# A hybrid decoder trunk in float32: more input projections multiply high and low tokens as one operand, in a new order, and the group norm's steps come later

## The chip, the cores and the metric

One core of a Trainium2 chip runs the whole kernel. The metric is the device time in microseconds (us), the median of the runs shown; lower is better.

## The reference

Two layers of width 1024 work on a sequence of 256 tokens. Each layer normalises the stream, projects it to 12,832 columns, and feeds three branches of 1024 channels: a Mamba-2 scan, a sliding-window attention and a forgetting attention. Each branch is multiplied by the SiLU of a gate of its own and projected back; the three are merged by sigmoid gates, projected once more and added to the stream.

```python
for layer in range(DEPTH):
    h = rms_norm(x, norm_w[layer])
    proj = einsum('bsd,de->bse', h, w_in[layer])
    (a_xbc, a_z, a_dt, b_q, b_k, b_v, b_z, c_q, c_k, c_v, c_f, c_z, gates) = split(proj)
    y_a = mamba2_branch(a_xbc, a_z, a_dt, ...)      # ends in grouped_rms_norm(y * silu(a_z))
    y_b = sliding_window_branch(rope(b_q), rope(b_k), b_v, b_z, ...)
    y_c = forgetting_attention_branch(c_q, c_k, c_v, c_f, c_z, ...)
    g = sigmoid(gates + gate_bias[layer])
    x = x + einsum(sum_i g_i * (y_i @ w_proj[layer, i]), w_out[layer])
return rms_norm(x, final_norm_w)
```

## The kernel before

**Numbers in two parts.** Everything is float32. So that TensorE can take its faster float32 form (fp32r), each number a is written as a high part, a rounded by ScalarE (ACT), and a low part, a - high, by VectorE (DVE); `split` (lines 261 to 268) does both. A product is then high x high + low x high + high x low, with the product of the two low parts left out.

**Weights.** SyncE loads 512 KB of weights at a time (128 partitions x 1024 columns, a "part") into six raw buffers. `feed` (357) splits a part into `hi` and `lo`, up to four parts ahead of TensorE (PE), and `release` (377) lets the next one in. A piece of 256 output columns is two parts: four of the eight 128-row blocks k each (`kper` is 4). It gives two blocks of 128 channels, u or half 0 and 1.

**Two ways to multiply 128 channels with 256 tokens.** The normalised tokens stand in `y.hT`, high and low side by side; `y.hTh` and `y.hTl` are views of its halves.
- `chan` (443) does for each of eight k three matmuls of 256 columns into one half of a PSUM bank: `hi` with the high tokens, `lo` with the high tokens, `hi` with the low tokens (`dense`, 278). That is 24 matmuls. The callers read the result from PSUM.
- `chan_sum` (450) loads `hi(k)` once and streams high and low tokens as one operand of 512 columns, so that the bank holds hi x high in the first half and hi x low in the second; `lo(k)` with the high tokens is added into the first half. That is 16 matmuls. Then ACT copies the second half to SBUF (line 463) and DVE adds the first (464). Its matmuls alternate: high 0, low 0, low 1, high 1, low 2, high 2 and so on.

`chan_sum` serves the queries of the sliding window but for the first group (`u_bq`, 536, through `rotated`, 499), the keys and queries of the forgetting attention (`u_ck`, `u_cq`), all its gates, and the first four gate blocks of branch 1 (`u_z`, 813). `chan` serves the sliding keys (`u_bk`), the first queries (g = 0), gate blocks u = 4 to 7 of branch 1, all eight gate blocks of the scan (branch 0) and the convolution's inputs.

**What is done with them.** `rotated` multiplies each half with the cosine and sine table (513), POOL adds or subtracts. `u_z` makes a SiLU: tanh of half the value on ACT (831, or 821 after `chan_sum`), then DVE's (1 + tanh) x value (834, 838, 823). For the scan, DVE then multiplies it with the scan's output `y.xs` (839), ACT squares it (841), and each second block adds two squares (844) and launches a group norm.

**The group norm** (849) has two steps on PE. The first sums the squares over channels with four small matmuls against `ones` (852); DVE, POOL and DVE again make the reciprocal root (854 to 866); ACT writes it as diagonal matrices (`diagonals`, 872). That writing is hung on the next `finish`, that is behind the next block's ACT instruction. The second step broadcasts the diagonals with two matmuls (882), DVE scales (885), and `split` makes the operand of the branch's projection.

**What sets the order.** PE's order is the order in which the program issues it. A modelled clock adds up matmul columns; multi-step work (`launch`, 103) waits in a list until its due time on that clock, and `pump` (130), called after each block, lets due steps in. The group norm's first step is due `D_GN1` after its gate block, the second `D_GN2` after the first. `drain` forces what is left of a branch's steps. The order on ACT, DVE and POOL is made by a scheduler from dependencies; each engine then runs its queue in that order. PSUM has three banks for these products ("mm") and five for the rest ("mx").

**Order of a layer.** Values, sliding keys, four groups of queries; branch 1's gates, the convolution's inputs and the forgetting attention's values, with attention steps in between; branch 1's merge gates and projection; more keys, queries and gates; then the scan's eight gate blocks u0 to u7, four blocks of merge gates (24 matmuls of 512 columns each), and the scan's projection, which needs the group norms.

Of the kernel before, what the change touches and what calls it, by code (L numbers as in the profile page):

```python
# [16 lines left out]
P = 128  # L17
# [6 lines left out]

D_SOFT, D_SOFT2, D_EVAC, D_SSD, D_SSD2 = 7.0, 3.0, 3.0, 8.0, 3.0
D_K, D_Q, D_QK, D_G0, D_FOX, D_BDMA, D_BIAS, D_BC, D_SSD3 = 6.0, 5.5, 2.0, 8.0, 0.0, 4.0, 2.6, 5.5, 1.0
D_GN1, D_GN2, D_CUM, D_H, D_M = 6.0, 9.0, 12.0, (4.8, 6.4), 5.0
BUDGET = 1.35
T_PP, T_SSD, T_BIAS = 1, 1, 1
N_RAW, N_SPLIT = 6, 6  # L30
# [14 lines left out]
def hybrid_trunk(  # L45
# [45 lines left out]
    def mm(o, a, b, **kw):  # L91
        n = b.free_size()
        if a.dtype == F32R:
            clock["t"] += max(0.094, n / 2350.0)
        else:
            clock["t"] += max(0.2, n / 587.0) * (0.5 if a.free_size() == 64 or a.shape[0] == 32 else 1.0)
        nc.tensor.matmul(o, a, b, **kw)  # L97
# [149 lines left out]
    def tokens_in_turn(a, k):  # L247
        return a[:, :, k, :].rearrange("p a i -> p i a")
# [5 lines left out]
    def halves(ap):  # L254

        return ap.rearrange("p (a i) -> p a i", a=2)
# [193 lines left out]
    def chan_sum(y, w, c, out):  # L450


        p = pmm()
        for k in range(NK):
            if k > 0:
                mm(p[:, 0:S], w.lo(k)[:, c:c + P], tokens_in_turn(y.hTh, k), start=False, stop=False)
            mm(p, w.hi(k)[:, c:c + P], y.hT[:, :, :, k, :].rearrange("p h a i -> p h i a"),
               start=(k == 0), stop=(k == NK - 1))
            if k == 0:
                mm(p[:, 0:S], w.lo(k)[:, c:c + P], tokens_in_turn(y.hTh, k), start=False, stop=False)  # L460
            if w.last and (k + 1) % w.kper == 0:
                release(w, k // w.kper + 1)
        finish(act(halves(out), ordered(p[:, S:2 * S]), AF.Copy))  # L463
        tt(halves(out), ordered(p[:, 0:S]), halves(out), op=ALU.add)  # L464

# [30 lines left out]

    def rotated(y, done, both):

        held = {}

        def u(half):
            def f(w):
                if both:
                    p = T("L1", [P, S])
                    chan_sum(y, w, half * P, p)
                    p = halves(p)
                else:
                    p = chan(y, w, half * P)  # L510
                for i in (half, 1 - half):
                    m = held[half, i] = T("L1", [P, S])
                    tt(halves(m), p, halves(cs[:, i, :]), op=ALU.mult)
                if half == 1:
                    done(held)
                pump()
            return f
        return u(0), u(1)
# [6 lines left out]
    def u_bk(y):  # L525

        def done(held):
            y.kT = T("L8", [P, 4, 2, S])
            add_rotated(y.kT[:, 0, :, :], held)
            for d in range(1, 4):  # L530
                m = 32 * d
                nc.gpsimd.dma_start(y.kT[m:P, d, :, :], y.kT[0:P - m, 0, :, :])
                nc.gpsimd.dma_start(y.kT[0:m, d, :, :], y.kT[P - m:P, 0, :, :])
        return rotated(y, done, False)

    def u_bq(y, g):

        def done(held):
            q = T("qt", [P, 2, S])
            add_rotated(q, held)  # L540
            launch(1, swa_quad(y, g, q), D_Q)
        return rotated(y, done, g > 0)

    def attn_quad(pair, products, biases, nsink, v, vcols, sz, gated, scored=lambda: None):

# [267 lines left out]
    def u_z(y, br, u, c):  # L813
        def f(w):
            if u == 0 and br != 0:
                y.sz[br] = T("L8", [P, NK, S])
            if br == 2 or br == 1 and u < 4:
                o = y.sz[br][:, u, :]
                chan_sum(y, w, c, o)
                th = T("L1", [P, S])  # L820
                act(th, o, AF.Tanh, scale=0.5)
                y.zdone.add((br, u))
                stt(o, th, 1.0, o, op0=ALU.add, op1=ALU.mult)
                pump()
                return
            p = chan(y, w, c)
            if u == 0 and br == 0:
                y.yh[br] = T("L8", [P, 2, NK, P], F32R)
                y.yl[br] = T("L8", [P, 2, NK, P], F32R)
            th = T("L1", [P, S])  # L830
            finish(act(halves(th), p, AF.Tanh, scale=0.5))
            y.zdone.add((br, u))
            if br != 0:
                stt(halves(y.sz[br][:, u, :]), halves(th), 1.0, p, op0=ALU.add, op1=ALU.mult)
            else:
                drain(0)
                sz = T("L1", [P, S])
                stt(halves(sz), halves(th), 1.0, p, op0=ALU.add, op1=ALU.mult)
                tt(y.xs[:, u, :], y.xs[:, u, :], sz, op=ALU.mult)
                sq = T("L1", [P, S])  # L840
                act(sq, y.xs[:, u, :], AF.Square)
                y.sq.append(sq)
                if u % 2 == 1:
                    tt(y.sq[-2], y.sq[-2], y.sq[-1], op=ALU.add)
                    launch(3 if u < 4 else 4, group_norm(y, u // 2, y.sq[-2]), D_GN1)
            pump()
        return f
# [596 lines left out]
```

## Time and profile before

| what | value |
|---|---|
| runs | 832.01, 829.56, 830.33 us; median 830.33 |
| the profiled execution | 830.05 us, of it span 828.2 (first to last instruction) |
| granted TensorE clock | 0.997 |
| ACT busy | 522.7 us (63%) |
| POOL busy | 97.3 us (12%) |
| HBM | 154.63 MB read, 189 GB/s over the span |

A row of groups reads: line of the kernel, engine, operation, written <- read, shapes, count; then busy time, mean ns of one, and the idle time of the engine ahead of it with what ended it. A matmul's duration is its way through the array, so that matmuls overlap; what one costs in a stream is the distance from start to start. A timeline row begins with start and length in us. PEld is the loading of weights, beside the matmuls.

### The profile page before, as it was taken

Reading aid. Unit: us, or ns where it says so; the run is one execution under the profiler, and the core shown is the slowest. Engines: PE = TensorE matmul, PEld = TensorE weight load, DVE = VectorE, ACT = ScalarE, POOL = GpSimd, SP = SyncE. Lnnn points to the kernel's source line nnn. Section 1 sums busy time; section 2 is a strip of 40 time slices with the busy share of each in tenths; the row PEclk is TensorE's granted clock in tenths of the full one; section 3 lists DMA queues with packets and bytes.
Section 4 is the critical chain, followed back from the end, with each engine's and each line's share of the span. In section 5 each row is a group of like instructions: output and inputs, shape, how many; then the busy total and the mean of one; then the engine's idle time right before and its main releaser. Section 6 shows DMA issues by size and latency. Waiting matters only on the chain.

```text
span 828.2 us, 15796 instructions
## 1 busy us (share of the span) xinstructions
PE 818.4 (99%) x5781; PEld 743.7 (90%) x5781; DVE 676.0 (82%) x1486; ACT 522.7 (63%) x1082; POOL 97.3 (12%) x150
## 2 busy tenths in 40 slices
PE   8999999999999999999999999999999999999996
PEld 8989999988888998888999999989888889888896
DVE  6998998797997778665788989988889778795665
ACT  7767777664676767353664687767557667664442
POOL 3340000000111010210004200000002110103000
PEclk9999999999999999999999999999999999999998
DMA  9876555766655555775688455756756555476632
GB/s 312 266 206 187 164 159 152 239 214 197 191 172 172 154 167 177 251 241 184 211 269 257 131 174 176 205 158 204 248 174 196 179 167 156 136 230 228 216 104 74
DMA packets 129558, 159.38 MB, mean 192 GB/s; under 512 B 7970, under 2 KB 98202, under 8 KB 129482
## 3 DMA queue, kind: packets, MB, share of 16 engines
q1 hardware_dynamic: 114960, 140.53, 54.1%
q10 hardware_dynamic: 13690, 16.24, 6.6%
q0 software_dynamic: 832, 1.62, 0.7%
q8 instruction: 45, 0.74, 0.4%
q14 instruction: 31, 0.25, 0.1%
HBM read 154.63 MB, written 2.16 MB: 189 GB/s over the span
## 4 chain that ended last, share of the span: by engine, by line
PE 90%; DVE 4%; issue 2%; DMA 2%; ACT 1%; SPq 0%; POOLq 0%; POOL 0%; DVEq 0%; ACTq 0%
PE mm L97 79%; PE mx L97 8%; PE mx L101 4%; DVE lo L265 1%; DMA L<-cumd 1%; DMA L<-in_x_dram 1%; DVE L L723 0%; ACT hi L264 0%; DVE L L265 0%; ACT L L872 0%; DVE pp L567 0%; DVE L L259 0%; DVE L L774 0%; DVE lo L259 0%; DVE pp L585 0%
## 5 line engine op out<-in xcount | busy, mean ns | idle before, releaser
L97 PE MATMUL mm<-L,hi 128*128 128x256 f32 (+1 forms) x1568 | 362.1, 316 | 0.0
L265 DVE TENSOR_TENSOR lo<-raw,hi 128x1024 fp32r<-128x1024 f32 (+2 forms) x276 | 314.8, 1157 | 51.9 <-ACT hi L264 48.6
L264 ACT ACTIVATE hi<-raw 128x1024 fp32r<-128x1024 f32 (+2 forms) x276 | 265.8, 980 | 96.0 <-PE mm L97 83.5
L97 PE MATMUL mm<-hi,L 128*128 128x512 f32 (+2 forms) x1232 | 323.7, 352 | 0.6 <-DVE qt L464 0.4
L97 PE MATMUL mm<-L,lo 128*128 128x256 f32 x1056 | 278.3, 274 | 0.0
L97 PEld LDWEIGHTS mm<-L,hi 128*128 128x128 f32 x1568 | 258.5, 191 | 18.1 <-issue 5.1
L97 PEld LDWEIGHTS mm<-hi,L 128*128 128x128 f32 x1232 | 216.7, 190 | 24.3 <-issue 0.7
L97 PE MATMUL mm<-lo,L 128*128 128x512 f32 (+2 forms) x616 | 213.7, 349 | 0.0
L97 PEld LDWEIGHTS mm<-L,lo 128*128 128x128 f32 x1056 | 202.5, 192 | 2.8
L97 PEld LDWEIGHTS mm<-lo,L 128*128 128x128 f32 x616 | 116.4, 190 | 11.5
L936 POOL TENSOR_SCALAR_AFFINE_SELECT bias<-bias 128x128 f32<-128x128 f32 x64 | 31.0, 520 | 394.9 <-DMA bias<-cumd 377.3
L573 ACT ACTIVATE pp<-pp,nm 128x128 f32<-128x128 f32 (+1 forms) x128 | 56.5, 443 | 17.2 <-DVE nm L567 17.2
L723 DVE SCALAR_TENSOR_TENSOR L<-L,vec,L 128x255 f32<-128x255 f32 (+2 forms) x96 | 46.2, 481 | 3.8 <-ACT L L720 2.5
L585 DVE TENSOR_SCALAR pp<-pp,rsum 128x128 f32<-128x128 f32 (+1 forms) x128 | 32.2, 315 | 0.5
L463 ACT ACTIVATE L<-mm 128x256 f32<-128x256 f32 x36 | 13.7, 381 | 26.5 <-PE mm L97 26.0
L967 ACT ACTIVATE L<-L 128x512 f32<-128x512 f32 x24 | 15.1, 628 | 20.4 <-DVE L L966 20.4
L604 ACT ACTIVATE L<-mx 128x512 f32<-128x512 f32 x48 | 26.7, 596 | 0.3
L101 PE MATMUL mx<-ident,pp 128*128 128x128 f32 x192 | 26.3, 273 | 0.0
L727 ACT ACTIVATE L<-L 128x256 f32<-128x256 f32 x32 | 13.4, 418 | 18.6 <-DVE L L723 10.6
L966 DVE TENSOR_TENSOR L<-mm,L 128x512 f32<-128x512 f32 x24 | 16.4, 684 | 9.4 <-PE mm L97 8.2
L573 ACT ACTIVATION_READ_ACCUMULATOR pp<-pp,nm 128x1 f32 x128 | 24.0, 187 | 0.0
L567 DVE CUSTOM_DVE_ANT_0 pp<-mx,wmask,nsink 128x128 f32<-128x128 f32 x64 | 23.4, 411 | 0.0
(203 smaller groups left out, 767.4 us busy)
## 6 DMA issues: line engine op xcount, KB each, us to landing
raw<-in_w_in_dram SPq DMA_DIRECT2D x191, 512.0 KB, 4.7
raw<-in_w_proj_dram SPq DMA_DIRECT2D x48, 512.0 KB, 5.1
raw<-in_w_out_dram SPq DMA_DIRECT2D x16, 512.0 KB, 5.0
bias<-cumd ACTq DMA_DIRECT2D x16, 256.0 KB, 3.6
L<-cumd ACTq DMA_DIRECT2D x8, 512.0 KB, 8.0
L<-in_gate_bias_dram ACTq DMA_DIRECT2D x12, 256.0 KB
raw<-in_w_in_dram SPq DMA_DIRECT2D x4, 408.0 KB
raw<-in_w_in_dram SPq DMA_DIRECT2D x4, 384.0 KB
```

Of the source, the lines that this page charges most:

```text
L97: nc.tensor.matmul(o, a, b, **kw)
L101: nc.tensor.transpose(o, a, i)
L264: keep(act)(hi, src, AF.Copy)
L265: keep(tt)(lo, src, hi.bitcast(F32), op=ALU.subtract)
L567: nc.vector.tensor_tensor_reduce(out=pp[:, i, sl], in0=score(p, i, b), in1=biases(p, i, b), scale=-0.125, scalar=1.0e30 if ns is None else ...
L573: act(pp[:, i, sl], pp[:, i, sl], AF.Exp, scale=-1.0, bias=nm[:, e:e + 1], accum_out=sums[:, e:e + 1])
L585: ts(pp[:, i, sl], pp[:, i, sl], rs[:, 2 * i + b:2 * i + b + 1], 0.5, op0=ALU.mult, op1=ALU.mult)
L604: act(pT, pt, AF.Copy)
L723: stt(a[:, s:S], x_[:, 0:S - s], y.vec[:, 16 * j + u:16 * j + u + 1], a[:, s:S], op0=ALU.mult, op1=ALU.add)
L936: nc.gpsimd.affine_select(out=bias[:, i, dst], in_=bias[:, i, src], compare_op=ALU.is_ge, fill=NEG, base=0, pattern=[[-1, P]], channel_mul ...
L966: tt(halves(g), p, halves(y.gb), op=ALU.add)
L967: finish(act(g, g, AF.Tanh, scale=0.5))
```

## The change

`chan_sum` issues its matmuls in another order: the high ones of the first part, all eight low ones, the high ones of the second part. `rotated` and `u_z` use `chan_sum` throughout, so that the sliding keys, the first queries, the last gates of branch 1 and the scan's gates no longer use `chan`; only the convolution's inputs do. In `u_z` tanh and the product read the sum in SBUF. `D_GN1` and `D_GN2` go from 6.0 and 9.0 to 8.5 and 9.5.

```diff
-D_GN1, D_GN2, D_CUM, D_H, D_M = 6.0, 9.0, 12.0, (4.8, 6.4), 5.0
+D_GN1, D_GN2, D_CUM, D_H, D_M = 8.5, 9.5, 12.0, (4.8, 6.4), 5.0
...
         p = pmm()
-        for k in range(NK):
-            if k > 0:
+        ks = range(NK)
+        high = [(k, True) for k in ks]
+        low = [(k, False) for k in ks]
+
+        m = w.kper
+        seq = high[:m] + low + high[m:]
+        done = [0] * len(w.parts)
+        for n, (k, h) in enumerate(seq):
+            if h:
+                mm(p, w.hi(k)[:, c:c + P], y.hT[:, :, :, k, :].rearrange("p h a i -> p h i a"),
+                   start=(n == 0), stop=(n == len(seq) - 1))
+            else:
                 mm(p[:, 0:S], w.lo(k)[:, c:c + P], tokens_in_turn(y.hTh, k), start=False, stop=False)
-            mm(p, w.hi(k)[:, c:c + P], y.hT[:, :, :, k, :].rearrange("p h a i -> p h i a"),
-               start=(k == 0), stop=(k == NK - 1))
-            if k == 0:
-                mm(p[:, 0:S], w.lo(k)[:, c:c + P], tokens_in_turn(y.hTh, k), start=False, stop=False)
-            if w.last and (k + 1) % w.kper == 0:
-                release(w, k // w.kper + 1)
+            done[k // m] += 1
+            if w.last and done[k // m] == 2 * m:
+                release(w, k // m + 1)
         finish(act(halves(out), ordered(p[:, S:2 * S]), AF.Copy))
         tt(halves(out), ordered(p[:, 0:S]), halves(out), op=ALU.add)
...
-    def rotated(y, done, both):
+    def rotated(y, done):
...
-                if both:
-                    p = T("L1", [P, S])
-                    chan_sum(y, w, half * P, p)
-                    p = halves(p)
-                else:
-                    p = chan(y, w, half * P)
+                p = T("L1", [P, S])
+                chan_sum(y, w, half * P, p)
                 for i in (half, 1 - half):
                     m = held[half, i] = T("L1", [P, S])
-                    tt(halves(m), p, halves(cs[:, i, :]), op=ALU.mult)
+                    tt(m, p, cs[:, i, :], op=ALU.mult)
...
-        return rotated(y, done, False)
+        return rotated(y, done)
...
-        return rotated(y, done, g > 0)
+        return rotated(y, done)
...
             if u == 0 and br != 0:
                 y.sz[br] = T("L8", [P, NK, S])
-            if br == 2 or br == 1 and u < 4:
-                o = y.sz[br][:, u, :]
-                chan_sum(y, w, c, o)
-                th = T("L1", [P, S])
-                act(th, o, AF.Tanh, scale=0.5)
-                y.zdone.add((br, u))
-                stt(o, th, 1.0, o, op0=ALU.add, op1=ALU.mult)
-                pump()
-                return
-            p = chan(y, w, c)
-            if u == 0 and br == 0:
+            elif u == 0:
                 y.yh[br] = T("L8", [P, 2, NK, P], F32R)
                 y.yl[br] = T("L8", [P, 2, NK, P], F32R)
+            o = T("L1", [P, S]) if br == 0 else y.sz[br][:, u, :]
+            chan_sum(y, w, c, o)
             th = T("L1", [P, S])
-            finish(act(halves(th), p, AF.Tanh, scale=0.5))
+            act(th, o, AF.Tanh, scale=0.5)
             y.zdone.add((br, u))
-            if br != 0:
-                stt(halves(y.sz[br][:, u, :]), halves(th), 1.0, p, op0=ALU.add, op1=ALU.mult)
-            else:
+            if br == 0:
                 drain(0)
-                sz = T("L1", [P, S])
-                stt(halves(sz), halves(th), 1.0, p, op0=ALU.add, op1=ALU.mult)
-                tt(y.xs[:, u, :], y.xs[:, u, :], sz, op=ALU.mult)
+            stt(o, th, 1.0, o, op0=ALU.add, op1=ALU.mult)
+            if br == 0:
+                tt(y.xs[:, u, :], y.xs[:, u, :], o, op=ALU.mult)
                 sq = T("L1", [P, S])
```

## The prediction

> **What bounds the kernel now.** I read the page first (busy shares, slices, the chain that ended last), then the chain in order of time, then PE's timeline where that chain leaves the matmuls, and last the DVE and ACT timelines in front of those places.
>
> ```profile
> span 828.2 us, 15796 instructions
> PE 818.4 (99%) x5781; PEld 743.7 (90%) x5781; DVE 676.0 (82%) x1486; ACT 522.7 (63%) x1082; POOL 97.3 (12%) x150
> PE   8999999999999999999999999999999999999996
> DVE  6998998797997778665788989988889778795665
> PE 90%; DVE 4%; issue 2%; DMA 2%; ACT 1%; SPq 0%; POOLq 0%; POOL 0%; DVEq 0%; ACTq 0%
> ```
>
> PE is busy from end to end and 90% of the chain is PE. So two things count: what one matmul costs in the stream (start to start), and the few places where PE stands still. DVE, at 82%, is the engine that could become late; ACT, at 63%, is less likely to.
>
> The chain in order of time (start, length, what) gives the cost in the stream. These pieces have no other work between their matmuls:
>
> ```profile
> 26.75 26.46 PE mm L97 x192
> ...
> 66.71 5.36 PE mm L97 x48
> ...
> 248.82 5.24 PE mm L97 x32
> ...
> 325.30 46.62 PE mm L97 x216
> ```
>
> The piece of 48 is two `chan` blocks, 24 matmuls of 256 columns each: 5.36 / 48 = 111.7 ns a matmul, 2.68 us a block. The piece of 32 is two `chan_sum` blocks, each with 8 matmuls of 512 and 8 of 256 columns: 2.62 us a block, 327.5 ns a pair. The piece of 216 is gates and projections, all 512 wide: 46.62 / 216 = 215.8 ns. And 215.8 + 111.7 = 327.5. So in this kernel a 512 costs 215.8 and a 256 costs 111.7, and the pair in `chan_sum` is just their sum. The piece of 192 holds the sliding keys, the first queries (four `chan`) and three more pairs of queries (six `chan_sum`): 4 x 2.68 + 6 x 2.62 = 26.44 of its 26.46 us, so PE waits for nothing there.
>
> How many blocks there are is read from PE's groups kept apart by form:
>
> ```profile
> L97 PE MATMUL mm<-L,lo 128*128 128x256 f32 x1056 | 278.3, 274 | 0.0
> ...
> L97 PE MATMUL mm<-L,hi 128*128 128x512 f32 x544 | 183.9, 387 | 0.0
> L97 PE MATMUL mm<-L,hi 128*128 128x256 f32 x1024 | 180.2, 278 | 0.0
> ```
>
> 544 / 8 = 68 blocks are `chan_sum`, 1024 / 16 = 64 are `chan`. Where PE does stand still is the third group norm of each layer:
>
> ```profile
> 318.53 0.38 PE L97 MATMUL mm<-lo,L 128*128 128x512 f32 x1
> 318.91 0.38 PE L97 MATMUL mx<-L,ones 128*128 128x256 f32 x1
> 319.49 0.39 PE L97 MATMUL mx<-L,ones 128*128 128x256 f32 x1 [0.20 <-ACT L L872]
> 319.71 0.60 PE L97 MATMUL mm<-hi,L 128*128 128x512 f32 x2
> ...
> 324.68 0.38 PE L97 MATMUL mm<-lo,L 128*128 128x512 f32 x1
> 324.90 0.40 PE L97 MATMUL mx<-L,ones 128*128 128x256 f32 x2
> 325.14 0.59 PE L97 MATMUL mm<-hi,L 128*128 128x512 f32 x2
> ...
> 724.35 0.38 PE L97 MATMUL mm<-lo,L 128*128 128x512 f32 x1
> ...
> 725.52 0.59 PE L97 MATMUL mm<-hi,L 128*128 128x512 f32 x2
> ```
>
> The fourth norm passes undisturbed: 324.68 to 325.14, 0.46 us from the gate's matmul before it to the one behind it. The third takes 318.53 to 319.71 = 1.18, and in the second layer 724.35 to 725.52 = 1.17. So 0.72 and 0.71 us are waiting, for the diagonals that ACT writes in L872.
>
> **The change, part by part.**
>
> **1. Sixteen blocks a layer from `chan` to `chan_sum`.** Two for the sliding keys, two for the first queries, four last gates of branch 1, eight gates of the scan: 32 in all. Each drops 8 of 24 matmuls, and 8 of 256 plus 8 of 256 become 8 of 512; the columns stay the same. Saved: 2.68 - 2.62 = 0.06 a block, 32 x 0.06 = 1.9 us. All of it is on PE's path.
>
> **2. The new order in `chan_sum`** (four high, eight low, four high) meets all 100 blocks. If each width keeps its price, it costs nothing, and that is the value I take, since 512s in an unbroken run (215.8), 256s in an unbroken run (111.7) and the alternation (327.5) add up. No row shows this exact order, so the bounds. The 327.5 of a pair could also be shared by columns, 218.3 and 109.2. If the 512s kept 218.3 while the lows in a run went to 111.7, a block would cost 8 x (218.3 + 111.7) = 2.64, 0.02 more, or 2.0 us over 100 blocks. If the lows kept 109.2 and the 512s went to 215.8, it would be 2.60, 0.02 less, or -2.0 us. The first half of the weights is released after eight matmuls as before, the low half of the first part is needed three highs (3 x 215.8 = 0.65 us) later; neither adds a wait.
>
> The Trainium skill ("TensorE: Matmul & The Clock Gate", Back-to-back issue gap and LDWEIGHTS) gives a warm gap of N/2.4 + 2.5 ns and P/1.2 = 107 ns for loading 128 columns, so that only columns would count. The 512s agree (215.8 by it), the 256s don't (109.2 by it, 111.7 here). By it part 1 would be worth 8 x (3 x 109.2 - 215.8 - 109.2) = 21 ns a block, an estimate of 0.7 us.
>
> **3. What DVE and ACT get for it.** Each of the 32 blocks now has ACT's copy (L463) and DVE's add (L464) ahead of what followed before; the products and tanh then read SBUF.
>
> ```profile
> L464 DVE TENSOR_TENSOR L<-mm,L x36: 400/416/425, 41.8 to 685.9; 128x256 f32<-128x256 f32 x36
> ```
> ```profile
> L463 ACT ACTIVATE L<-mm 128x256 f32<-128x256 f32 x36 | 13.7, 381 | 26.5 <-PE mm L97 26.0
> ```
>
> 32 x 0.42 = 13.3 us more on DVE, 32 x 0.38 = 12.2 on ACT. I cost this at nothing, because PE's stream covers it. How thin the cover is, by stretch (length; PE, PEld, DVE, ACT, POOL busy):
>
> ```profile
> 20.00:42.00 22.00, 22.00 (x186) 21.63 (x185) 21.84 (x37) 17.34 (x37) 7.71 (x12) 1.00 0.90 269
> 42.00:54.00 12.00, 12.00 (x74) 10.81 (x73) 11.76 (x20) 6.75 (x13) 5.05 (x4) 1.00 0.86 231
> 279.00:307.00 28.00, 28.00 (x261) 26.75 (x260) 23.40 (x67) 18.91 (x48) 2.17 (x2) 1.00 0.49 151
> ```
> ```profile
> 27.92 3.09 DVE L265 TENSOR_TENSOR lo<-raw,hi 128x512 fp32r<-128x512 f32 x5
> ```
>
> At the keys and first queries DVE has no idle time left, and four adds (1.7 us) come in. But the lows run ahead: the five in the last row are ready by 31.01, and the last one belongs to the second queries, which PE reaches at 26.75 + 4 x 2.68 = 37.5. Six microseconds of lead against 1.7. In the scan's gates (279 to 307) DVE has 28.0 - 23.4 = 4.6 us idle and gets 8 x 0.42 = 3.4. If that cover were gone, each microsecond of lateness would be one of time.
>
> **4. Group norm steps later** (8.5 and 9.5 for 6.0 and 9.0). In the order in which the changed program's instructions stand on PE, the four sums, which stood behind the scan's gates u4, u5, u7 and behind the first merge gate, now stand behind u5, u6, u7 and half a merge gate (12 matmuls) later; the products with `ones` of norms one, two and four move back by 12 such matmuls each. The third norm's products stay 48 gate matmuls behind its sums. No DMA is in these steps. So the wait can only go if ACT comes sooner:
>
> ```profile
> 313.39 3.42 ACT L264 ACTIVATE L<-L 128x256 fp32r<-128x256 f32 x8 [2.51 <-DVE L L885]
> ...
> 317.66 0.61 ACT L967 ACTIVATE L<-L 128x512 f32<-128x512 f32 x1
> 318.18 0.97 ACT L872 ACTIVATE L<-ident,sm 128x128 fp32r<-128x128 f32 x3
> ...
> 319.06 0.38 ACT L872 ACTIVATE L<-ident,sm 128x128 fp32r<-128x128 f32 x1
> ```
> ```profile
> 316.19 0.68 DVE L966 TENSOR_TENSOR L<-mm,L 128x512 f32<-128x512 f32 x1
> 316.79 0.15 DVE L854 TENSOR_SCALAR sm<-mx 128x4 f32<-128x4 f32 x1
> 318.15 0.16 DVE L859 TENSOR_TENSOR sm<-sm,sm 128x4 f32<-128x4 f32 x1 [1.21 <-POOL sm L857]
> ...
> 318.74 0.17 DVE L865 CAST sm<-rs 128x4 fp32r<-128x4 f32 x1
> ```
>
> The diagonals stand behind the first gate's tanh (L967, 317.66), which waits for its DVE add (316.19), which stands behind the scaling and splits of norms one and two; ACT has eight splits there too. In the changed order that add stands ahead of norm two's scaling, and the tanh and the third diagonals ahead of its splits. That takes two scalings and two low splits (four operations of the shape of L464's, some 1.7 us of DVE) and two high splits (2 x 3.42 / 8 = 0.9 of ACT) from in front of diagonals that are 0.72 late. Both waits go: -1.43 us. What is late next: the third norm's sums need the squares of u4 and u5, and DVE now stands at the second norm's sums (behind u6 on PE) before it may add up u5. Queued behind that read are u5's add, whose PSUM bank u7 takes (about 0.5 + 0.15 + 0.42 = 1.1 us after the sums, and u7 begins 3.2 after them), and the rest of u5's work. From those sums: 0.5 for the matmuls, 2.1 from L854 to L865 (316.79 to 318.91), then the gate's product, L866, one value product (L627), the product with the scan, ACT's square and the adding of squares, 0.42 + 0.16 + 0.68 + 0.42 + 0.42 + 0.42 = 2.5, with 0.42 for each of that shape: 5.1 us, by an estimate 5.3 with the gaps between engines. PE takes
>
> ```profile
> 298.37 0.51 PE L97 MATMUL mx<-ones,L 128*128 128x2 f32 x4
> ...
> 301.55 0.38 PE L97 MATMUL mm<-L,hi 128*128 128x256 f32 x1
> ```
> ```profile
> 303.08 0.68 DVE L627 TENSOR_TENSOR L<-mx,L 128x512 f32<-128x512 f32 x1
> ```
>
> 3.18 from sums over value products to the next block, and 2.62 for it: 5.8. About half a microsecond is left.
>
> **Sum.** -1.9 + 0 + 0 - 1.43 = -3.4 us. The profiled execution took 830.05 (span 828.2 and 1.85 around it), so 826.7 for it; it stands 0.28 below the median of 830.33. For the median: **826.9**.
>
> **Rivals.**
> *Only columns count, or the order costs.* If the streamed columns alone set the time, part 1 brings nothing; if it brings its 1.9 and the order costs the upper bound of part 2, the two make +0.1. With the 1.43 either way 828.9 to 829.0. For it: the columns are the same. Against it: 5.36 and 5.24 for the same columns, and the sum 215.8 + 111.7. (The skill's rule in part 2 leaves part 1 an estimated 0.7, which gives 828.2; the trace's 256s, 2.5 ns dearer than by it, speak against it.)
> *The lows in a run are fast.* Low weights behind low weights might go at 109.2. Against it: 111.7 holds over 48 in a row, high behind high and low behind high. 826.9 - 2.0 = 824.9.
> *The wait stays or moves.* The third diagonals keep their distance to the sums on PE; if ACT's order doesn't help, only 1.9 is gained: 828.4.
> *DVE becomes the bound in the scan's gates* (slower). DVE stands idle at the first and second norm's sums, which now come a block later, while its 3.4 us of added work queue behind: the half microsecond at the third sums is used up and the third diagonals stay late. It decides when DVE is more than 0.5 us behind there. Fully unabsorbed: 2 x (3.4 - 0.5) = +5.8, and the 1.43 isn't gained: 830.33 - 1.9 + 5.8 = 834.2. For it: 23.4 of 28 busy and waits in DVE's order; against it: PE waits on nothing of DVE's today where DVE is fullest (20 to 54).
>
> **How the numbers follow.** Forecast 0.50, columns or order 0.15, fast lows 0.10, wait stays 0.12, DVE bound 0.13. What a measurement of this kernel can tell from no change is about 0.3%, 2.5 us: faster means below 827.8, slower above 832.8. Forecast (all but a tail of 0.04) and fast lows are faster: 0.56. Columns or order, the wait that stays and that tail are the same: 0.31. DVE bound: 0.13. The range takes in fast lows (824.9) and the cases from 828.4 to 829.0 with a part of a late DVE: 824.6 to 829.6; it leaves out most of the slow case.
>
> **What would show it.** Blocks of 16 matmuls at 2.62 us where 24 stood at 2.68, and 2.62 still for ck and cq (2.64 or 2.60 decides part 2). 0.46 in place of 1.18 around the third norm's products. No idle PE before the sums with `ones`. DVE fuller from 279 to 307, with no PE wait on L464's line. It would be wrong if PE waits for a low weight, for a PSUM bank behind a late add, or at the third sums.

## The result and the profile after

| kernel | median (lowest to highest) | runs |
|---|---|---|
| before | 830.25 us (829.56 to 832.01) | 6 |
| after | 833.54 us (832.41 to 835.36) | 6 |

The change makes the kernel slower by 0.4%: ratio 1.0041, 95% interval 1.003 to 1.0052. The profiled execution of after took 835.36 us (span 833.6), the slowest of its six, so its rows show somewhat more loss than the median has.

Lines of the page of after that answer to the first ones shown of before:

```profile
PE 818.7 (98%) x5525; PEld 732.3 (88%) x5525; DVE 689.4 (83%) x1518; ACT 531.8 (64%) x1114; POOL 99.8 (12%) x150
...
DVE  6999998797997788866789999988989778896665
...
PE 64%; DVE 20%; ACT 6%; issue 5%; DMA 2%; POOL 1%; SPq 0%; POOLq 0%; DVEq 0%; ACTq 0%
```

The first two lines hardly tell a difference: 13.4 us more DVE work, 83% for 82%. The last one does. PE carried 90% of the chain that ended last and carries 64% now; DVE went from 4% to 20%. What made PE stand still is in the list of PE's waits of after (who waited for whom: us in total, times, longest):

```profile
PE mm L97 <- DVE qt L471: 2.6, 3, 1.8
PE mx L97 <- DVE L L837: 1.7, 2, 0.9
...
PE mx L101 <- DVE pp L588: 1.1, 2, 0.5
...
PE mm L97 <- DVE L L471: 0.4, 1, 0.4
```

The two left out (2.0 us) fall in the kernel's first 10 us. The four shown are PSUM banks behind a late add of halves (L471), the adding of squares ahead of the third norm's sums (L837), and the softmax of the window attention (L588). Not one is a low weight, the only thing of DVE's whose lead the prediction had worked out.

**The stream did what was forecast.** Two `chan_sum` blocks in the chain of after, one scan's gate block in PE's timeline (start, length; eight highs that run over a block's border, then eight lows, then four highs), and the groups by form:

```profile
231.58 5.24 PE mm L97 x32
```
```profile
297.80 1.89 PE L97 MATMUL mm<-L,hi 128*128 128x512 f32 x8
299.53 1.05 PE L97 MATMUL mm<-L,lo 128*128 128x256 f32 x8
300.42 1.03 PE L97 MATMUL mm<-L,hi 128*128 128x512 f32 x4
```
```profile
L97 PE MATMUL mm<-L,hi 128*128 128x512 f32 x800 | 202.6, 385 | 1.8 <-DVE qt L471 1.8
L97 PE MATMUL mm<-L,hi 128*128 128x256 f32 x512 | 91.2, 278 | 0.4 <-DVE L L471 0.4
```

800 / 8 = 100 blocks are `chan_sum` now, 512 / 16 = 32 are `chan`. A block costs 5.24 / 2 = 2.62 us in the new order as in the old, eight highs 299.53 - 297.80 = 1.73 (216 ns each), eight lows 0.89 (111 ns). The Trainium skill ("TensorE: Matmul & The Clock Gate", Back-to-back issue gap) would have 109.2 for the 256s, an estimate from its N/2.4 + 2.5; the lows in a run are above that too.

**The third norm's products pass undisturbed**, 317.63 to 318.09 = 0.46 us where before had 1.18:

```profile
317.63 0.38 PE L97 MATMUL mm<-lo,L 128*128 128x512 f32 x1
317.85 0.40 PE L97 MATMUL mx<-L,ones 128*128 128x256 f32 x2
318.09 0.59 PE L97 MATMUL mm<-hi,L 128*128 128x512 f32 x2
```

### The profile page after: what moved, and what is told of

Same layout as the page of the kernel before. It is cut to its first block, busy times and chain, and to the rows that moved or that the text cites. A ratio compares the mean times of both kernels' runs of the same rounds, so it can differ in the third digit from the quotient of the medians.

```text
span 833.6 us, 15340 instructions
## 1 busy us (share of the span) xinstructions
PE 818.7 (98%) x5525; PEld 732.3 (88%) x5525; DVE 689.4 (83%) x1518; ACT 531.8 (64%) x1114; POOL 99.8 (12%) x150
## 4 chain that ended last, share of the span: by engine, by line
PE 64%; DVE 20%; ACT 6%; issue 5%; DMA 2%; POOL 1%; SPq 0%; POOLq 0%; DVEq 0%; ACTq 0%
PE mm L97 56%; DVE lo L265 8%; PE mx L97 5%; DVE L L726 3%; PE mx L101 2%; ACT hi L264 2%; ACT pp L576 2%; DMA L<-cumd 2%; DVE L L471 1%; DVE pp L588 1%; POOL sm L850 1%; DVE L L516 1%; DVE pp L570 1%; DVE L L731 1%; DVE L L630 1%
## 5 line engine op out<-in xcount | busy, mean ns | idle before, releaser
L264 ACT ACTIVATE hi<-raw 128x1024 fp32r<-128x1024 f32 (+2 forms) x276 | 265.5, 980 | 76.0 <-PE mm L97 60.1
L97 PE MATMUL mm<-L,hi 128*128 128x512 f32 (+1 forms) x1312 | 292.4, 343 | 2.1 <-DVE qt L471 1.8
L97 PEld LDWEIGHTS mm<-L,hi 128*128 128x128 f32 x1312 | 218.9, 191 | 24.1 <-issue 4.4
L97 PE MATMUL mm<-L,lo 128*128 128x256 f32 x1056 | 175.8, 275 | 0.0
L97 PEld LDWEIGHTS mm<-L,lo 128*128 128x128 f32 x1056 | 153.9, 191 | 5.5
L929 POOL TENSOR_SCALAR_AFFINE_SELECT bias<-bias 128x128 f32<-128x128 f32 x64 | 26.5, 450 | 401.5 <-DMA bias<-cumd 386.0
L470 ACT ACTIVATE L<-mm 128x256 f32<-128x256 f32 x68 | 25.5, 375 | 37.8 <-PE mm L97 36.4
L471 DVE TENSOR_TENSOR L<-mm,L 128x256 f32<-128x256 f32 x68 | 28.3, 416 | 6.0 <-ACT L L470 5.4
L826 ACT ACTIVATE L<-L 128x256 f32<-128x256 f32 x48 | 19.8, 412 | 20.6 <-DVE L L471 20.6
L588 DVE TENSOR_SCALAR pp<-pp,rsum 128x128 f32<-128x128 f32 (+1 forms) x128 | 32.2, 315 | 0.5
L830 DVE SCALAR_TENSOR_TENSOR L<-L,L 128x256 f32<-128x256 f32 x48 | 20.3, 422 | 10.1 <-ACT L L826 10.1
L101 PEld LDWEIGHTS mx<-ident,pp 128*128 128x128 f32 x192 | 22.4, 141 | 4.1 <-DVE pp L588 1.9
```

The source lines that it names most:

```text
L101: nc.tensor.transpose(o, a, i)
L264: keep(act)(hi, src, AF.Copy)
L588: ts(pp[:, i, sl], pp[:, i, sl], rs[:, 2 * i + b:2 * i + b + 1], 0.5, op0=ALU.mult, op1=ALU.mult)
L929: nc.gpsimd.affine_select(out=bias[:, i, dst], in_=bias[:, i, src], compare_op=ALU.is_ge, fill=NEG, base=0, pattern=[[-1, P]], channel_mul ...
```

## Where the time went

The best base is a kernel with the new order and the later norm steps but no block converted (below, 827.8 us). With PE's blocks of it and of after laid side by side, after falls behind at these places (profiled executions):

| place in after, us | what PE waits for | lost, us |
|---|---|---|
| 70.4 | PSUM bank, first convolution block (layer 0 only) | 0.53 |
| 138.1, 547.2 | softmax of the window attention (L588) | 1.16, 1.16 |
| 163.3 | bank behind an add of ck/cq (layer 0 only; behind a DMA) | 1.93 |
| 175.3, 582.4 | the same, later | 0.66, 0.66 |
| 311.9, 718.9 | squares for the third norm's sums (L837) | 1.02, 1.02 |

Together 8.1 us. The stream's gain of 32 x 0.06 = 1.9 comes off, and smaller steps, 0.5 us of them in the first 10 us of the kernel, add 1.4: that is the spans' difference of 7.65. Of these waits only that at 175.3 stands in before, and there 0.37 us long:

```profile
170.57 0.70 PE L97 MATMUL mm<-hi,L 128*128 128x512 f32 x2 [0.37 <-DVE qt L464]
```

**The softmax** shows how they arise. First before, the last two gates of branch 1 (u6, u7): DVE's rows, then ACT's (start, length; in brackets idle time and who ended it):

```profile
120.18 0.41 DVE L834 SCALAR_TENSOR_TENSOR L<-L,mm 128x256 f32<-128x256 f32 x1
...
121.98 0.42 DVE L834 SCALAR_TENSOR_TENSOR L<-L,mm 128x256 f32<-128x256 f32 x1
123.11 1.23 DVE L265 TENSOR_TENSOR lo<-raw,hi 128x1024 fp32r<-128x1024 f32 x1 [0.72 <-ACT hi L264]
```
```profile
120.78 0.38 ACT L831 ACTIVATE L<-mm 128x256 f32<-128x256 f32 x1 [0.19 <-PE mm L97]
```

u7's tanh (L831) waits for nothing but PE, 0.19 us, and neither product (L834) waits; DVE stands idle only behind them, 0.72 us for a high split (L264). After, the same two gates:

```profile
122.86 0.42 DVE L471 TENSOR_TENSOR L<-mm,L 128x256 f32<-128x256 f32 x1
...
123.76 0.42 DVE L830 SCALAR_TENSOR_TENSOR L<-L,L 128x256 f32<-128x256 f32 x1 [0.15 <-ACT L L826]
124.71 1.23 DVE L265 TENSOR_TENSOR lo<-raw,hi 128x1024 fp32r<-128x1024 f32 x1 [0.53 <-ACT hi L264]
125.85 0.42 DVE L471 TENSOR_TENSOR L<-mm,L 128x256 f32<-128x256 f32 x1
126.75 0.43 DVE L830 SCALAR_TENSOR_TENSOR L<-L,L 128x256 f32<-128x256 f32 x1 [0.48 <-ACT L L826]
127.70 1.23 DVE L265 TENSOR_TENSOR lo<-raw,hi 128x1024 fp32r<-128x1024 f32 x1 [0.53 <-ACT hi L264]
```
```profile
123.31 0.42 ACT L826 ACTIVATE L<-L 128x256 f32<-128x256 f32 x1 [0.99 <-DVE L L471]
123.63 1.04 ACT L264 ACTIVATE hi<-raw 128x1024 fp32r<-128x1024 f32 x1
124.58 0.37 ACT L470 ACTIVATE L<-mm 128x256 f32<-128x256 f32 x1
...
126.30 0.42 ACT L826 ACTIVATE L<-L 128x256 f32<-128x256 f32 x1 [0.38 <-DVE L L471]
```

Read them as a chain between two queues. ACT's tanh (L826) waits 0.99 and 0.38 us for DVE's add (L471). Behind the tanh in ACT's queue stands the high split of the next weights (L264). DVE, its add done, waits for the tanh (0.15, 0.48) and then for that high split (0.53 twice). u7's last four high matmuls are through on PE at 121.00 + 1.03 = 122.03, but ACT's copy of the sum (L470) starts only at 124.58, behind the tanh of u6 and a high split. Each such place, where one engine's queue stands until another's has come to a result, is called a handoff or crossing here; a converted gate has two more of them (copy to add, add to tanh). The row of these matmuls:

```profile
121.00 1.03 PE L97 MATMUL mm<-L,hi 128*128 128x512 f32 x4
```

DVE's idle time doesn't take up the added 0.42 us per block. From 10 us before PE's scores to the softmax that reads them (length; PE, PEld, DVE, ACT, POOL busy) DVE is idle for 13.78 - 12.23 = 1.55 us before, and for 16.22 - 14.32 = 1.90 after:

```profile
116.69:130.47 13.78, 13.78 (x133) 13.04 (x132) 12.23 (x21) 10.52 (x19) 1.23 (x4) 1.00 0.88 256
```
```profile
117.97:134.19 16.22, 16.22 (x134) 14.81 (x133) 14.32 (x25) 11.58 (x22) 1.30 (x4) 1.00 0.82 246
```

The lateness is measured from PE's scores to DVE's first softmax instruction, before and then after:

```profile
126.69 1.59 PE L97 MATMUL mx<-L,qt 32*128 32x128 f32 x32
...
130.47 0.35 DVE L567 CUSTOM_DVE_ANT_0 pp<-mx,wmask,nsink 128x128 f32<-128x128 f32 x1
```
```profile
127.97 1.59 PE L97 MATMUL mx<-L,qt 32*128 32x128 f32 x32
...
134.19 0.34 DVE L570 CUSTOM_DVE_ANT_0 pp<-mx,wmask,nsink 128x128 f32<-128x128 f32 x1
...
138.08 1.27 PE L101 MATMUL mx<-ident,pp 128*128 128x128 f32 x6 [0.55 <-DVE pp L588]
```

3.78 us became 6.22, and the transposes of `pp` that hang on it are late: 2.44 us of lateness cost PE 1.16, so by an estimate some 1.3 us were slack.

**At 163.3** a DMA comes in between. ACT issues the scan's DMA (L751); DVE's L767 stands idle for it, and the add that frees PE's bank is queued behind L767:

```profile
153.84 0.94 ACTq L751 DMA_DIRECT2D L<-cumd  x2
```
```profile
161.54 0.16 DVE L767 TENSOR_TENSOR ds<-L,acum 128x4 f32<-128x4 f32 x1 [4.82 <-DMA L<-cumd]
161.65 1.23 DVE L265 TENSOR_TENSOR lo<-raw,hi 128x1024 fp32r<-128x1024 f32 x1
162.79 0.42 DVE L471 TENSOR_TENSOR qt<-mm,qt 128x256 f32<-128x256 f32 x1
```

In the base the same DMA is issued at 150.94, the idle time is 2.52 and PE doesn't wait. Of the 2.9 us by which it is issued later 1.6 are PE's own delay by then; and the data come 7.7 us behind the issue (161.54 - 153.84) for 5.4 there (156.34 - 150.94). The later issue alone doesn't make PE wait. In the run with the scan's gates back on `chan` (below) the DMA is issued at nearly the same time as in after, DVE has its data 5.5 us later (159.17 - 153.66), and PE doesn't wait here:

```profile
153.66 0.94 ACTq L751 DMA_DIRECT2D L<-cumd  x2
```
```profile
159.17 0.16 DVE L767 TENSOR_TENSOR ds<-L,acum 128x4 f32<-128x4 f32 x1 [2.63 <-DMA L<-cumd]
```

Over the runs here this way takes from 5.0 to 8.3 us, for which none gives the reason. Without the 1.93 the profiled execution would stand 7.65 - 1.93 = 5.7 us above the base, as the medians do (below); so by an estimate this wait is what makes it slower than the median.

## The experiments

Ratios are to runs of before on the same chip, with their 95% intervals. A difference in us between two experiments is one of medians, some of them from different chips; taken from the ratios it comes out up to 0.7 us otherwise. First the parts alone.

**The new order alone.**
```diff
-        for k in range(NK):
...
+        seq = high[:m] + low + high[m:]
...
+        for n, (k, h) in enumerate(seq):
```


> The kernel before with only the new order of the matmuls in chan_sum (four high, eight low, four high); the blocks that use chan keep it, the group norm keeps its due times. My theory now: VectorE, with an add more for each of 32 blocks, is late at places where PE waits for a softmax, a PSUM bank or a square; the order costs nothing. By it this run stays at 830.2, within 0.7. Rival, the order itself costs (the low weights one behind the other, 100 blocks in the changed kernel, 68 here): 832 or more.


829.09 us, 0.9985 (0.9977 to 0.9994): 1.15 better, where nothing was expected. The block price is unchanged; the gain is waits (in each layer one group of scores is 0.5 us shorter, and the bank wait at 170.57, which cost 0.5, is gone). Why the order does that was not settled.

**The later norm steps alone.**
```diff
-D_GN1, D_GN2, D_CUM, D_H, D_M = 6.0, 9.0, 12.0, (4.8, 6.4), 5.0
+D_GN1, D_GN2, D_CUM, D_H, D_M = 8.5, 9.5, 12.0, (4.8, 6.4), 5.0
```


> The kernel before with only D_GN1 and D_GN2 at 8.5 and 9.5. By the theory of a late VectorE the third norm's squares are in time here, since VectorE has no added work, and at most the 1.4 us of the third norm's products go: 828.8 to 830.2, with no wait of PE on the adding of squares. Rival, the later steps themselves bring the wait at the third sums (1.03 us a layer in the changed kernel): 831 to 832.5.


828.31, 0.998 (0.9971 to 0.999): the 1.43 of the third norm and the same 0.5 at 170 us.

**Both, no block converted** (the base from here on).


> The kernel before with the new order in chan_sum and with the later group norm steps; no block goes from chan to chan_sum. If the two gains add up (829.09 and 828.31 against 830.24): 827.2. It would be the fastest so far. If they win back the same waits: 828.3.


827.8 (827.23 to 829.18), 0.9972 (0.9962 to 0.9982), the fastest kernel of the study. It falls 0.6 short of the two gains added up, about the wait at 170 us that either part removes.

**The 32 blocks alone** (order and norm steps of before; the edit is shown against before), and then **after with the old norm steps**.
```diff
-            p = chan(y, w, c)
+            o = T("L1", [P, S]) if br == 0 else y.sz[br][:, u, :]
+            chan_sum(y, w, c, o)
...
-        return rotated(y, done, g > 0)
+        return rotated(y, done)
```


> The 32 blocks go to chan_sum, but with the old order inside it and the old due times of the group norm. By the theory of a late VectorE: -1.9 us of stream, and about 2.3 us at the softmax behind the last gates of branch 1, 2.5 at the PSUM banks of the first keys and queries of the forgetting attention, 0.5 at the first convolution block come on top: 832.5 to 834. Rivals (order or group norm): the stream's gain shows, 828.3.


```diff
-D_GN1, D_GN2, D_CUM, D_H, D_M = 8.5, 9.5, 12.0, (4.8, 6.4), 5.0
+D_GN1, D_GN2, D_CUM, D_H, D_M = 6.0, 9.0, 12.0, (4.8, 6.4), 5.0
```


> The changed kernel with D_GN1 and D_GN2 back at 6.0 and 9.0. By the theory of a late VectorE the group norm decides little: the waits at the softmax and at the banks stay, so 832.5 to 834. Rival, the later group norm steps are what costs: 831.5 or less.


842.89 (1.0145, 1.0126 to 1.0165) and 841.34 (1.012, 1.0098 to 1.0143), far beyond every expectation. PE's longest wait is for the squares of the norm in both:

```profile
PE mx L97 <- DVE L L830: 7.6, 4, 2.8
```
```profile
PE mx L97 <- DVE L L837: 6.0, 4, 2.1
```

With the blocks converted the norm's sums come too early, and the later steps are worth 7.8 us there (841.34 to 833.54), not the 1.9 that they gain alone.

So from the base the blocks lose 833.54 - 827.8 = 5.7 us though the stream gains 1.9: some 7.7 us of waits. Which blocks?

**After with the scan's gates back on `chan`, and with the last gates of branch 1 back** (tanh and product from PSUM again). The first edit is shown; in the second the condition is `br == 1 and u >= 4`.
```diff
+            if br == 0:
+                p = chan(y, w, c)
+                th = T("L1", [P, S])
+                finish(act(halves(th), p, AF.Tanh, scale=0.5))
...
+            else:
...
                 chan_sum(y, w, c, o)
```


> The changed kernel with the scan's eight gates a layer back on chan. Its 16 blocks give back 1.0 us of stream, the wait at the third sums (2 x 1.03) should go: 832 to 832.5. If more than the waits that PE shows there hang on these gates: under 831.

> The changed kernel with branch 1's last four gates a layer back on chan. Its 8 blocks give back 0.5 us of stream; the waits at the softmax (2 x 1.16), at the banks behind it (1.93 and 0.66) and at 115 us (0.23) should go: 833.5 + 0.5 - 5.1 = 829. If those waits come from the keys and first queries far ahead of them: 833 to 834.


832.47 (1.0021, 1.0009 to 1.0033) and 829.95 (0.9996, 0.9987 to 1.0004). Without the scan's gates the waits for the squares are gone. The 1.93 at 163.3 is gone too, but these gates come later in the layer than 163 us; as said, the DMA took less long. Without the eight last gates (four in each layer) the softmax waits and all waits of ck/cq are gone: 3.6 us for 8 of the 32 blocks.

**Only one group converted, on the base:** first the keys and first queries, then the last gates.
```diff
-        return rotated(y, done, False)
+        return rotated(y, done, True)
...
-        return rotated(y, done, g > 0)
+        return rotated(y, done, True)
```


> The order in chan_sum and the later group-norm steps, and of the 32 blocks only the 8 of the sliding keys and first queries converted. If the lead of the lows covers their work, as the prediction had it: 827.3 (827.8 less 8 times 0.06 us). If each block costs its share of the 7.7 us (8/32): 829.2.


```diff
-            if br == 2 or br == 1 and u < 4:
+            if br != 0:
```


> The same base, and of the 32 blocks only the 8 last gates of branch 1 converted. Taking them back out of the changed kernel gained 3.6 us (833.54 to 829.95). If they cost that by themselves, through the softmax and the adds behind them: 831.4. If they cost it only on top of the other blocks' work: 827.3 to 828.5.


828.82 (0.998, 0.9969 to 0.9991): 1.0 above the base, nearer to the share of 829.2 than to the covered 827.3, but the interval overlaps the base's (0.9962 to 0.9982), so that a cost of these 8 blocks isn't shown. In the trace PE waits 1.5 us for banks behind adds, the one at 70 us among them. And 832.18 (1.0022, 1.0013 to 1.0032): the last gates cost 4.4 us by themselves, at the places of after and, but for the one behind the DMA, in its sizes (1.16 at the softmax in both layers; 1.06, 0.66 and 0.66 at ck/cq).

**Load or handoff?** On the base, an in-place VectorE maximum in each of the 32 blocks (behind the tanh of a gate, behind the first product with the table in the 8 others) gives the load of the add without a new crossing. An in-place ScalarE copy behind it makes the way to and fro in the 24 gates. In the third run, shown against the second, that copy works on a table that nothing waits for.
```diff
             finish(act(halves(th), p, AF.Tanh, scale=0.5))
+            tt(th, th, th, op=ALU.max)
```


> As e8_order_and_norm, chan kept in the 32 blocks, but with one more VectorE operation of 128x256 in each (the maximum of a tile with itself, in place, which leaves the values as they are). Theory of VectorE's load (13 us more work is what makes it late): about as late as in the changed kernel, that is 827.2 and up to 8, 832 to 835. Rival, the longer chain ScalarE, VectorE, ScalarE, VectorE of chan_sum is what makes things late, not the amount of work: 827 to 829.


```diff
+            tt(th, th, th, op=ALU.max)
+            act(th, th, AF.Copy)
```


> The 32 blocks keep the summed (two-pass) form of before, the order in the 8 other groups and the later group-norm steps stay, and each of the 32 blocks has one more in-place VectorE maximum (as in the run of one more VectorE operation, 831.86); the 24 gate blocks of them get one in-place ScalarE copy behind it as well, so that a gate block goes ScalarE, VectorE, ScalarE, VectorE as in the changed kernel. What it leaves out: nothing; it adds operations that change no value. Theory 'the added VectorE work alone is late, about 4 us of 7.7': 831.9, and below 833.0 for the ScalarE work. Theory 'the longer way to and fro between ScalarE and VectorE makes the other half': 835.5 (827.8 + 7.7; the 1.95 us of the faster stream are not in it), and not below 834.


```diff
-            act(th, th, AF.Copy)
+            act(cs[:, 0, :], cs[:, 0, :], AF.Copy)
```


> As the run 'there and back' (836.05), but the additional ScalarE operation of the 24 gate blocks copies a constant table in place and not the tanh, so that the work added on VectorE and ScalarE is the same and no value's way crosses from ScalarE to VectorE and back once more. If the crossing is what made the 4.2 us between 831.86 and 836.05: 832 to 832.5. If ScalarE's added 24 x 0.4 us of work is: 835.5 to 836.5.


831.86 (1.0023, 1.0014 to 1.0032), 836.05 (1.007, 1.005 to 1.009) and 832.22 (1.0023, 1.0014 to 1.0032). The maximum alone costs 4.1 us, between the two theories' ranges. The copy in the chain costs 4.2 more, the same copy beside it 0.4: ScalarE has room for the work, not for the handoff. But in all three runs what PE mostly waits for is a PSUM bank (3.6, 7.0 and 3.7 us of its waits): the product there still reads PSUM, so that whatever stands ahead of it holds the bank longer. A converted block frees its bank at the add. The 4.1 and the 4.2 are therefore prices with the bank in them, not a split of what after loses.

**The same, in the 8 last gates alone**, where after loses most.
```diff
+            if br == 1:
+                tt(th, th, th, op=ALU.max)
```


> The order in chan_sum, the later group-norm steps, no block converted, and only in the 8 last gates of branch 1 one in-place VectorE maximum behind the tanh. With these 8 blocks converted the time was 832.18, 4.4 above the base of 827.8 although the stream is 0.5 shorter. If VectorE's additional 8 x 0.42 us of work does that: 832.2 to 832.7. If the crossing between ScalarE and VectorE is needed for it: 827.8 to 829.


```diff
+            if br == 1:
+                tt(th, th, th, op=ALU.max)
+                act(th, th, AF.Copy)
```


> As the run before it, and behind the maximum an in-place ScalarE copy of the tanh, so that these 8 gate blocks cross from ScalarE to VectorE and back once more. Crossing theory: 832.2 to 832.7 with TensorE's waits at the softmax of the attention and at the adds of cq, as with the 8 blocks converted. Load theory: no more than 0.5 above the run before it.


828.75 (0.9975, 0.9966 to 0.9985) and 832.25 (1.0021, 1.0011 to 1.003). Load costs 0.95, which by its interval can't be told from nothing; load and handoff 4.45; the conversion of these blocks 4.4, or 4.9 without the stream's gain of 0.5. With load alone DVE's idle time does take up the work (13.78 - 13.32 = 0.46 us are left of 1.55), and the softmax isn't later behind the scores (131.58 - 127.80 = 3.78, as before):

```profile
117.80:131.58 13.78, 13.78 (x133) 13.04 (x132) 13.32 (x22) 10.73 (x19) 2.25 (x4) 1.00 0.87 254
```
```profile
127.80 1.59 PE L97 MATMUL mx<-L,qt 32*128 32x128 f32 x32
...
131.58 0.34 DVE L574 CUSTOM_DVE_ANT_0 pp<-mx,wmask,nsink 128x128 f32<-128x128 f32 x1
```

With the blocks converted it is 133.24 - 127.03 = 6.21, as in after.

One part of the expectation failed. With the copy added, PE's main wait is not at the softmax but for the bank that the product holds over the whole way to and fro:

```profile
PE mm L97 <- DVE L L844: 3.3, 2, 1.6
```

So it is shown that load alone isn't what the last gates cost, and that a crossing put into such a chain is dear. For the converted blocks the rows of DVE and ACT show where it acts; how their 4.4 us would split between load and handoff without that bank is not shown.

**Ways out that weren't.** GpSimd does the add in the 32 blocks:
```diff
-        tt(halves(out), ordered(p[:, 0:S]), halves(out), op=ALU.add)
...
+            act(halves(top), ordered(p[:, 0:S]), AF.Copy)
+            gtt(out, out, top, op=ALU.add)
...
```


> The changed kernel, but in the 32 converted blocks ScalarE copies both halves out of PSUM and GpSimd adds them, so that VectorE gets no additional operation. Theory 'VectorE's load is the cause': 829.5 (833.5 less about 4 us). Theory 'the way to and fro is the cause' (ScalarE, GpSimd, ScalarE, VectorE is longer still): 833 or more.


846.51 (1.0187, 1.0171 to 1.0204). Less load on DVE, a longer chain (GpSimd's add takes 0.84 us by its row, DVE's 0.42), and 13 us worse than after. ACT gets 32 more copies too, which this run doesn't keep apart:

```profile
L474 POOL TENSOR_TENSOR L<-L,L 128x256 f32<-128x256 f32 x32 | 26.8, 840 | 219.6 <-ACT L L473 219.6
```

Four PSUM banks for the products:
```diff
-        return PS("mm", 3)
+        return PS("mm", 4)
...
-        return PS("mx", 5)
+        return PS("mx", 4)
```


> The changed kernel with four PSUM banks for the products and four for the rest, in place of three and five. If PE's waits for a bank whose add is late are 3 us of the lost time: 830.5, and no wait of TensorE for VectorE's add of the two halves in the trace. If the late VectorE only shows elsewhere: 833 or more (the four banks for the rest can also cost by themselves, which this run does not separate).


841.34 (1.013, 1.0117 to 1.0144). The waits for L471 and for the softmax's `pp` vanish, but with four banks for the rest the window attention's products with the values wait 6.4 us for the softmax to free one. The 1.7 us at the third sums stay as in after. So much else moves that the run doesn't price the bank waits.

The first norm's steps later still, in after, and with only the scan's gates converted on the base:
```diff
-D_GN1, D_GN2, D_CUM, D_H, D_M = 8.5, 9.5, 12.0, (4.8, 6.4), 5.0
+D_GN1, D_GN2, D_CUM, D_H, D_M = 11.0, 9.5, 12.0, (4.8, 6.4), 5.0
```


> The changed kernel with the steps of the first group norm planned at 11.0 us and not 8.5. If the waits of the third norm's sums for the squares (1.0 us in each layer) are what is left there: 831.5. If the wait only moves to the steps behind it: 832.5 or more.

> The order in chan_sum and the later group-norm steps, and of the 32 blocks only the 16 of the scan's gates converted, with the steps of the first norm at 11.0 us. If these 16 can be paid for in their place: 826.8 (827.8 less 16 times 0.06 us). If each converted block costs what it costs in the changed kernel (5.7 us for 32): 829 to 831.


834.0 (1.0045, 1.0027 to 1.0063) and 830.11 (0.9994, 0.9984 to 1.0004). The 1.02 at the third sums goes; some 0.9 us come back in each layer at the third norm's diagonals, as in before, and some 0.5 for a bank behind an add (L471) ahead of the sums. The 16 gates cost 2.3 us on the base, with these steps. The three groups, each alone on the base, make 1.0 + 4.4 + 2.3 = 7.7 us against 5.7 together, so they don't simply add up.

## Why the prediction was wrong

**Part 1 (the stream) was right:** 2.62 for 2.68 us a block, so that neither "only columns count" nor "the lows in a run are fast" came true. **Part 2 (the order) was right for the stream** (2.62), and left out a gain of about a microsecond in waits. Its premise was off: in the alternation of before the 327.5 ns of a pair are shared as 218 for the 512 and 109 for the 256 (medians of 476 distances from start to start), the second split that it named, and in the new order as 216 and 112. The sum stayed; that both shares moved by as much is luck as far as the prediction goes, and no run says why. **Part 4's -1.43 was right** for the third norm's products, which no longer wait.

**The step that failed is part 3:** "I cost this at nothing, because PE's stream covers it." It checked two covers. One was the lead of the low weights, and that held: PE waits for no low weight. But the add doesn't only delay the lows. It sends each gate block from ACT to DVE and back once more, and what is queued behind it on either engine comes late: adds that free banks, the softmax, squares. Two of the signs of being wrong that the prediction named, a PSUM bank behind a late add and the third sums, are what the trace shows. The other cover was DVE's idle time in a stretch (4.6 us against 3.4 of added work). That idle time is mostly DVE waiting for someone (from 279 to 307 in before, 2.1 us for GpSimd's power and 2.0 for a high split), and ahead of the softmax the new handoffs brought more of it (1.90 us for 1.55). Part 3 looked at the keys and first queries and at the scan's gates; most was lost in the eight last gates of branch 1, a stretch it didn't look at, in front of a softmax with 1.3 us of slack. The missing term was +7.7 us; less the 1.1 that the order gained (827.8 for the 828.9 that the prediction has without part 1) it is the 6.6 between 826.9 and 833.54 (the prediction's own terms, added up unrounded, make 827.0).

**Part 4's second half failed by a size:** "About half a microsecond is left" at the third sums. PE arrives 6.08 us behind the second norm's sums (311.04 - 304.96; 5.8 forecast), and the squares are there after 6.95 (311.91 - 304.96; 5.3 forecast):

```profile
304.96 0.50 PE L97 MATMUL mx<-ones,L 128*128 128x2 f32 x4
...
311.91 0.58 PE L97 MATMUL mx<-ones,L 128*128 128x2 f32 x4 [0.87 <-DVE L L837]
```
```profile
304.29 1.97 POOL L850 TENSOR_TENSOR sm<-sm,mhalf 128x4 f32<-128x4 f32 x1 [28.88 <-DVE sm L847]
```
```profile
306.30 0.16 DVE L852 TENSOR_TENSOR sm<-sm,sm 128x4 f32<-128x4 f32 x1 [0.62 <-POOL sm L850]
...
307.38 0.15 DVE L847 TENSOR_SCALAR sm<-mx 128x4 f32<-128x4 f32 x1
```

The chain itself was well estimated: 311.91 - 307.38 = 4.53 from L847, against 5.3 - 0.5 = 4.8. But it starts 1.9 us late (sums done at 304.96 + 0.50 = 305.46, read at 307.38), since L847 of the second norm is queued behind the first norm's steps, and those wait for GpSimd's power (1.97 us). In before the same power took 1.06 with no work of DVE's beside it; here DVE's low split runs beside its first 1.05 us:

```profile
296.55 1.06 POOL L857 TENSOR_TENSOR sm<-sm,mhalf 128x4 f32<-128x4 f32 x1 [25.46 <-DVE sm L854]
```
```profile
304.12 1.22 DVE L265 TENSOR_TENSOR lo<-raw,hi 128x1024 fp32r<-128x1024 f32 x1
```

So some 0.9 of the 1.9 us go with that split, by an estimate from these two rows; it is as long as PE's wait here.

**The rival "DVE becomes the bound in the scan's gates"** had the sign, and 834.2 for 833.54, but not the mechanism: of the 7.7 us the third sums hold 2 x 1.02, and the diagonals' wait is gone all the same. Its size was a coincidence.

## What to carry to other kernels

Idle time of an engine that trades results with another is no room for added work as long as it isn't known what the idle time waits for. An instruction that puts one more crossing into such a chain can cost far more than its duration, since it is paid on both queues: here 3.5 us for 8 copies (828.75 to 832.25), a bank held longer included, where 24 copies beside the chain cost 0.4. When a step is added, list for each later consumer on both queues (banks to be freed, a softmax, DMAs issued from the queue) how long before its need it is ready now, in every stretch that gets the step. To price it, run the same instruction inside the chain and beside it.

## What was not expected of the hardware

- The same ScalarE copy, 24 times, cost 4.2 us in a chain with VectorE (the banks that it holds longer are most of it) and 0.4 beside it, with TensorE 98 to 99% busy in every one of these kernels.
- GpSimd's power on 128x4 took 1.97 and 1.94 us where VectorE's low split ran beside its first 1.05 to 1.07 us, and 1.01 to 1.06 where VectorE ran nothing beside it (before, 25.46 us of idle ahead or 5.82) or an add that reads PSUM (after, at 307.68). So idle time ahead isn't the reason.
- The same high and low matmul cost 327.5 ns together in both orders, but 218 and 109 in alternation and 216 and 112 in runs.
- The new order of matmuls, of the same price in the stream, was worth 1.15 us in waits.
